# Moving the operands of a matmul stream by 64 bytes: where `u`, the weight ring and the block sums lie modulo 256 bytes

## Chip, cores, metric

One core of a Trainium2 chip runs one program. The metric is the device time of one execution in microseconds; the time of a kernel is the median of its runs.

## What is computed

One layer of a decoder block on 512 tokens of width 1024, in float32, with three sub-layers that each start from a normalised and modulated `u`:

```python
mod = cond @ w_ada[l] + b_ada[l]
u = modulate(rmsnorm(h, g_norm_ffn1[l]), sh1, sc1)
h = h + 0.5 * gt1 * swiglu(u, w_ffn1_in[l], w_ffn1_out[l])
u = modulate(rmsnorm(h, g_norm_mix[l]), sh2, sc2)
h = h + gt2 * token_mixing(u, cos, sin, w_in[l], ...)      # pooling and dilated attention, gated
u = modulate(rmsnorm(h, g_norm_ffn2[l]), sh3, sc3)
h = h + 0.5 * gt3 * swiglu(u, w_ffn2_in[l], w_ffn2_out[l])
return rmsnorm(h, g_final)
```

`swiglu` is `(silu(u @ w1) * (u @ w2)) @ w_out` with an inner width of 2816 (22 tiles of 128). All matrices are float32.

## The kernel before, in words

Everything is kept transposed: features on the 128 partitions, the 512 tokens along the free dimension, so `h` and `u` are eight tiles of 128x512. Precision comes from splitting: every operand x is stored as a high part `hi` and a rest `lo` (type float32r), and a product is three matmuls into one PSUM bank: `hi·uh`, `hi·ul`, `lo·uh` (`mm3`, lines 323 to 325). The **stationary** operand of a matmul is a 128x128 weight tile, 512 bytes a partition, which a weight load brings in while the matmul before it runs; the **moving** operand is 512 or 256 columns of `u` (2048 or 1024 bytes a partition).

**The ring.** Weights come from HBM in chunks of mostly 128x1024 into `raw` buffers (or, for block sums of weights, `X`). ScalarE writes each chunk's high part into the ring `whi` (L280), VectorE the rest into `wlo` (L292). `plan` lists all chunks in the order of use; `room` gives each the next place in the ring, in pieces of 128 floats (`unit`): where a chunk runs over the ring's end, it is cut in two and each piece has its own two instructions. `look` keeps the splitting three or four chunks ahead of `take`, which hands the tiles to TensorE.

**Order of the work.** All queues are written out by hand. In time: the startup (`startup`, L1482 to 1486: eight k-tiles, each 8 banks x 3 matmuls of 512 columns); the first feed-forward layer (ffn1): four pairs of inner tiles with 512-column matmuls (`ffn_pair`), seven `duo`s, and after each of five parts a stretch of output matmuls over the products `HI`/`HK` (512 columns); the mixing layer (mix); the second feed-forward layer (ffn2).

A `duo` makes two pairs of inner tiles with seven block products (`product`, L710 to 712) in place of eight, by sums of blocks of `u` and of the weights. A product is 24 matmuls of 256 columns. The moving operands of the seven, in order: `UH`/`UL`, `S0`, `S1`, `UH`/`UL`, `S2`, `UH`/`UL`, `UH`/`UL`, where S0 to S2 are the sums of blocks of `u` (`SH`/`SL` in the trace), made once for each feed-forward layer.

At the seams between the layers the tokens go in two halves of 256 columns: `out_tail` makes the last output tiles of a layer (for all its `ms`, first the left half, then the right half with the same weights) while the next norm starts on the left half, and `head` makes the first four input tiles of the next layer in the same way. In between stand the norm's sum over features (`stats_t`, L409) and its spreading (`spread`, L419), both small matmuls. `out_end` is the same for the end of the program. These are the "half tiles".

**Where the operands lie.** Tiles of a pool lie one behind the other, so addresses follow from the order and the sizes. In the built program `whi` starts at byte 13440 and `wlo` at 42112 of a partition, both 128 modulo 256; the ring's length (7168 floats) and a weight tile (512 bytes) are multiples of 256, so **every weight tile lies at 128 modulo 256**. `HI`, `HK`, `MH`, `ML`, `PH`, `YH` (moving operands of output stretches) lie at 128. `UH` starts at 87616 and `UL` at 104768, both 64; 16 floats more are reserved in each, and `place_u` moves the views by `U_AT` floats when a layer's norm begins:

```python
U_AT = (0, 16, 0)      # layer 0: ffn1, 1: mix, 2: ffn2
```

So `u` lies at 64 in ffn1 and ffn2, and at 128 in mix. S0 lies at 128; a pad of 48 floats behind it puts S1 and S2 at 64. Below, "equal" means that the moving operand and the weights of a matmul have the same address modulo 256, "64 apart" that the moving operand lies 64 bytes before the weights.

Of the kernel before, what the change touches and what calls it, by code (L numbers as in the profile page):

```python
# [8 lines left out]
F32 = mybir.dt.float32  # L9
F32R = mybir.dt.float32r  # L10
# [4 lines left out]
P = 128  # L15
T = 512
HT = 256
D = 1024
KT = 8
# [91 lines left out]


FIRST = 4
RING = 7 * 1024


U_AT = (0, 16, 0)

PLAIN = {0: 8, 2: 4}
PARTS = ((0, 4), (4, 8), (8, 12), (12, 16), (16, 22))  # L120
# [3 lines left out]
def pairs_before(n, part):  # L124

    k1 = PARTS[part][1]
    return k1 if part + 1 == len(PARTS) or (n == 2 and part == 0) else k1 + 2


def chunk_widths():  # L130
    outs = [D] * (KT // 2 * (len(PARTS) - 1)) + [(FT - PARTS[-1][0]) * P] * KT
    f1 = [2 * FIRST * P] * KT + [D] * (2 * (FT - FIRST)), outs
    mix = [D] * 20 + [D, D] + [D, D, 4 * P] * (KT - 1) + [4 * P] + [D] * KT
    return f1, mix, ([D] * (2 * FT), outs)


class Kernel:
# [6 lines left out]
    def plan(self):  # L144
        (i1, o1), mix, (i2, o2) = chunk_widths()
        self.chunks = []
        for name, ws in (("wf1i", i1), ("wf1o", o1), ("wmix", mix), ("wf2i", i2), ("wf2o", o2)):
            off, rec = 0, []
            for w in ws:
                rec.append((name, off, w))  # L150
                off += P * w
            self.chunks.append(rec)
        f1i, f1o, mx, f2i, f2o = self.chunks


        self.loads, self.order, self.last = [], [], {}

        def plain(recs):
            for r in recs:
                n = len(self.loads)  # L160
                self.loads.append(r)
                self.last[n] = len(self.order)
                self.order.append((r[2], n, ("raw", n), None))

        def blocks(recs):
            n = len(self.loads)
            self.loads.extend(recs)
            r11, r12, r22, r21 = (("raw", n + i) for i in range(4))
            x0, x1 = ("x", 0), ("x", 1)
            for need, src, make in ((0, r11, None), (1, x0, (x0, r12, r11)), (2, x1, (x1, r22, x0)), (3, r21, None),  # L170
                                    (3, r12, (r12, r22, r12)), (3, r22, None), (3, x0, (x0, r21, x1))):
                for j, x in enumerate((r11, r12, r22, r21)):
                    if x == src or (make and x in make):
                        self.last[n + j] = len(self.order)
                self.order.append((D, n + need, src, make))

        def ffn(n, ins, outs, first):
            j, at = first, 0
            if first:
                plain(ins[:KT])  # L180
                at = KT
            for part, (k0, k1) in enumerate(PARTS):
                while j < pairs_before(n, part):
                    if j < PLAIN[n]:
                        plain(ins[at:at + 2])
                        j, at = j + 1, at + 2
                    else:
                        blocks(ins[at:at + 4])
                        j, at = j + 2, at + 4
                plain(outs[part * KT // 2:(part + 1) * KT // 2] if part + 1 < len(PARTS) else outs[-KT:])  # L190

        ffn(0, f1i, f1o, FIRST)
        base = len(self.order)
        plain(mx)
        ffn(2, f2i, f2o, 0)
        self.fetched = self.done = self.made = 0
        self.pos, self.held, self.retired, self.half = 0, None, [], None
        self.at, self.start, self.top = {}, {}, 0
        self.buf = {}
        self.units = {base + i: 2 * P for i in (4, 5)}  # L200
        self.units.update({base + i: T for i in range(16, 20)})
# [33 lines left out]
    def room(self, i, held):  # L235


        w, u, at, pieces = self.order[i][0], self.unit(i), self.top, []
        for c in range(0, w, u):
            if at % RING + u > RING:  # L240
                at += RING - at % RING
            o = at % RING
            if pieces and pieces[-1][0] + pieces[-1][1].stop - pieces[-1][1].start == o:
                pieces[-1] = (pieces[-1][0], slice(pieces[-1][1].start, c + u))
            else:
                pieces.append((o, slice(c, c + u)))
            at += u
        low = min((self.start[j] for j in range(held, i)), default=self.top)
        return (pieces, at) if at - low <= RING else None

# [201 lines left out]
        self.nc.vector.scalar_tensor_tensor(self.UL[k][:, hs], t[:, hs], S, self.UH[k][:, hs],  # L452
                                            op0=OP.add, op1=OP.subtract)

    def place_u(self, n):
        self.UHv, self.ULv = (x[:, U_AT[n]:U_AT[n] + KT * T] for x in (self.UHall, self.ULall))
        self.UH, self.UL = ([x[:, k * T:(k + 1) * T] for k in range(KT)] for x in (self.UHv, self.ULv))

    def norm_steps(self, n, hs):

        t, done = {}, [0]

        def upto(k):
            while done[0] <= min(k, KT - 1):
                i = done[0]
                if i == 0:
                    t[0] = self.norm_a(n, 0, hs)
                if i + 1 < KT:
                    t[i + 1] = self.norm_a(n, i + 1, hs)
                self.norm_b(n, i, hs, t.pop(i))  # L470
                done[0] += 1
        return upto
# [9 lines left out]
    def out_tail(self, ms, ksrc, gate, nxt, squares):  # L482


        nc = self.nc
        tiles, starts = {}, {}
        A, Bh = slice(0, HT), slice(HT, T)
        step = None
        self.held = self.pos
        for h, hs in enumerate((A, Bh)):  # L490
            for m in ms:
                bank = self.nb()
                if h == 0:
                    starts[m] = self.pos
                    tiles[m] = ksrc(m)
                    starts[m + 1] = self.pos
                if h == 0 and m == ms[0]:
                    nc.scalar.preload_act_table(AF.Sqrt)
                if self.done < self.pos + 4:
                    self.split_hi()  # L500
                ks = tiles[m]
                for i, (hi, lo, uh, ul) in enumerate(ks):
                    if h == 1 and m == ms[1] and i == 3:
                        self.stats_t(self.B[6], A)
                    if h == 1 and m == ms[2] and i == 1:
                        self.spread(self.B[6], A)
                        self.place_u(nxt)
                        step = self.norm_steps(nxt, A)
                        step(0)
                    self.mm3(bank[:, hs], hi, lo, uh[:, hs], ul[:, hs], i == 0, i == len(ks) - 1)  # L510
                s = squares(m)[:, :HT]
                self.tail_step(m, hs, bank, gate, s)
                if h == 1:
                    self.held = starts[m + 1]
                    if step:
                        step(1 if m != ms[-1] else 3)
                self.split_lo()
                nc.vector.tensor_tensor(self.acc[:, hs], self.acc[:, hs], s, op=OP.add)
                self.fetch()
        self.stepA = step  # L520
# [171 lines left out]
    def step(self):  # L692

        self.now += 1
        due = [f for t, f in self.put if t <= self.now]
        self.put = [x for x in self.put if x[0] > self.now]
        for f in due:
            f()
# [105 lines left out]
    def open_sums(self):  # L804
        st = ExitStack()
        bp = st.enter_context(self.tc.tile_pool(name="fs", bufs=1))
        self.S = []
        for i in range(3):
            self.S.append([bp.tile([P, 4 * HT], F32R, name=f"S{x}{i}") for x in "HL"])
            if i == 0:  # L810
                bp.tile([P, 48], F32, name="padb")
        self.S.append([x.rearrange("p (k t) -> p k t", k=KT)[:, :4, HT:] for x in (self.UHv, self.ULv)])
        return st

# [520 lines left out]
    def build(self):  # L1335
# [6 lines left out]
        tl = lambda n, w, dt=F32: per.tile([P, w], dt, name=n)  # L1342
        self.free = [tl(f"raw{i}", CW) for i in range(3)]

        self.hi, self.lo = tl("whi", RING, F32R), tl("wlo", RING, F32R)
        self.vecs = tl("vecs", 106)
        self.H = [tl(f"H{k}", T) for k in range(KT)]
        self.UHall = tl("UH", KT * T + 16, F32R)
        cst, self.eps = tl("cst", 163), tl("eps", 1)
        self.ULall = tl("UL", KT * T + 16, F32R)  # L1350
        self.place_u(0)
        self.AR = tl("AR", 2 * T)
        self.acc, self.R = self.AR[:, :T], self.AR[:, T:]
        self.mod, self.part = tl("mod", 72), tl("part", 1)
# [197 lines left out]
```

## Time and profile before

| | |
|---|---|
| median of 3 runs | 1021.69 us |
| the runs | 1021.69, 1025.06, 1021.38 us |
| profiled execution, own time | 1025.08 us |
| its span | 1023.3 us |
| its granted TensorE clock | 0.998 |
| matmuls | 6364, as many weight loads |

A "busy" figure adds up the time of instructions. A matmul's own duration is longer than its distance to the next one, since matmuls are pipelined: how fast a stretch goes is read from the distance between the starts of two matmuls and the number of matmuls from one to the other, which the code gives.

### The profile page before, as it was taken

How to read it: one execution, taken by the hardware profiler on the slowest of the kernel's cores; microseconds unless marked ns; L12 is line 12 of the kernel's file. 1: busy time of each engine (PE TensorE's matmuls, PEld its weight loads, DVE VectorE, ACT ScalarE, POOL GpSimd, SP SyncE). 2: the span in 40 equal slices, each digit the busy share in tenths (PEclk: the TensorE clock that was granted, in tenths of full speed). 3: DMA queues.
4: the chain of work that ended last, by engine and by line, in shares of the span. 5: the costliest groups of instructions: out<-in, count | busy, mean ns of one | idle time of the engine just before them, and what ended most of it. 6: DMA issues, size and time to landing. Idle time of an engine off the chain costs nothing.

```text
span 1023.3 us, 15508 instructions
## 1 busy us (share of the span) xinstructions
PE 1012.1 (99%) x6364; PEld 914.9 (89%) x6364; DVE 753.2 (74%) x1082; ACT 434.8 (42%) x638; POOL 26.0 (3%) x30
## 2 busy tenths in 40 slices
PE   8999999999999999999999999999999999999997
PEld 7888898989999899889988888998899899998997
DVE  6969879889786777779446776577787776676754
ACT  5453352534445552334314333454365354352552
POOL 0000000000000000006100000000000000000001
PEclk9999999999999999999999999999999999999999
DMA  8856365555533513222154774322244234241312
GB/s 315 285 177 256 112 238 162 172 162 188 165 115 106 157 35 103 62 83 83 32 185 156 268 263 127 104 63 72 94 155 135 83 103 145 84 144 45 112 32 83
DMA packets 43113, 139.60 MB, mean 136 GB/s; under 512 B 4897, under 2 KB 8225, under 8 KB 43042
## 3 DMA queue, kind: packets, MB, share of 16 engines
q1 hardware_dynamic: 42354, 137.95, 41.3%
q8 instruction: 50, 0.82, 0.3%
q10 hardware_dynamic: 688, 0.66, 0.2%
q14 instruction: 21, 0.17, 0.1%
HBM read 135.82 MB, written 2.77 MB: 135 GB/s over the span
## 4 chain that ended last, share of the span: by engine, by line
PE 95%; DVE 3%; DMA 1%; ACT 0%; issue 0%; DVEq 0%; ACTq 0%
PE bank L323 17%; PE bank L324 17%; PE bank L325 17%; PE bank L710 10%; PE bank L712 10%; PE bank L711 10%; PE bank L1486 1%; PE bank L1484 1%; PE bank L1482 1%; PE bank L1080 1%; PE bank L1259 1%; PE bank L1411 1%; PE bank L1260 1%; PE bank L1261 1%; PE bank L1028 1%; PE bank L1057 1%
## 5 line engine op out<-in xcount | busy, mean ns | idle before, releaser
L292 DVE TENSOR_TENSOR wlo<-raw,whi 128x1024 fp32r<-128x1024 f32 (+2 forms) x151 | 175.5, 1165 | 69.0 <-ACT whi L280 68.8
L280 ACT ACTIVATE whi<-raw 128x1024 fp32r<-128x1024 f32 (+2 forms) x151 | 150.4, 1003 | 42.6 <-DVE raw L228 39.8
L323 PE MATMUL bank<-UH,whi 128*128 128x512 f32 (+1 forms) x432 | 159.0, 368 | 0.0
L324 PE MATMUL bank<-UL,whi 128*128 128x512 f32 (+1 forms) x432 | 154.9, 359 | 0.2 <-DVE UL L452 0.2
L325 PE MATMUL bank<-UH,wlo 128*128 128x512 f32 (+1 forms) x432 | 154.9, 359 | 0.0
L323 PE MATMUL bank<-HI,whi 128*128 128x512 f32 (+1 forms) x406 | 146.8, 362 | 0.0
L324 PE MATMUL bank<-HK,whi 128*128 128x512 f32 (+1 forms) x406 | 146.5, 361 | 0.0
L325 PE MATMUL bank<-HI,wlo 128*128 128x512 f32 (+1 forms) x406 | 146.5, 361 | 0.0
L710 PE MATMUL bank<-UH,whi 128*128 128x256 f32 x512 | 141.6, 277 | 0.0
L711 PE MATMUL bank<-UL,whi 128*128 128x256 f32 x512 | 141.6, 277 | 0.0
L712 PE MATMUL bank<-UH,wlo 128*128 128x256 f32 x512 | 141.6, 277 | 0.0
L292 DVE TENSOR_TENSOR wlo<-X,whi 128x1024 fp32r<-128x1024 f32 (+2 forms) x88 | 104.4, 1188 | 39.5 <-ACT whi L280 39.3
L710 PE MATMUL bank<-SH,whi 128*128 128x256 f32 x384 | 107.1, 279 | 0.3 <-ACT u L717 0.3
L711 PE MATMUL bank<-SL,whi 128*128 128x256 f32 x384 | 106.9, 278 | 0.0
L712 PE MATMUL bank<-SH,wlo 128*128 128x256 f32 x384 | 106.9, 278 | 0.0
L280 ACT ACTIVATE whi<-X 128x1024 fp32r<-128x1024 f32 (+2 forms) x88 | 89.3, 1028 | 33.1 <-DVE X L228 32.1
L711 PEld LDWEIGHTS bank<-UL,whi 128*128 128x128 f32 x512 | 96.1, 188 | 0.3
L710 PEld LDWEIGHTS bank<-UH,whi 128*128 128x128 f32 x512 | 96.1, 188 | 0.3
L712 PEld LDWEIGHTS bank<-UH,wlo 128*128 128x128 f32 x512 | 96.4, 188 | 0.0
L325 PEld LDWEIGHTS bank<-UH,wlo 128*128 128x128 f32 x432 | 81.3, 188 | 12.8
L324 PEld LDWEIGHTS bank<-UL,whi 128*128 128x128 f32 x432 | 81.5, 189 | 12.3 <-issue 0.5
L323 PEld LDWEIGHTS bank<-UH,whi 128*128 128x128 f32 x432 | 81.4, 189 | 11.9 <-issue 0.5
(225 smaller groups left out, 1748.5 us busy)
## 6 DMA issues: line engine op xcount, KB each, us to landing
ada<-wada SPq DMA_DIRECT2D x47, 512.0 KB, 5.0
raw<-wmix SPq DMA_DIRECT2D x44, 512.0 KB, 3.9
raw<-wf1i SPq DMA_DIRECT2D x34, 512.0 KB, 4.5
raw<-wf2i SPq DMA_DIRECT2D x30, 512.0 KB, 3.6
X<-wf2i SPq DMA_DIRECT2D x14, 512.0 KB, 3.5
cs<-wada SPq DMA_DIRECT2D x12, 512.0 KB, 3.5
AR<-wada SPq DMA_DIRECT2D x12, 512.0 KB, 3.9
raw<-wf2o SPq DMA_DIRECT2D x12, 512.0 KB, 3.6
```

The source lines that it names most:

```text
L280: self.nc.scalar.activation(self.hi[:, y], r[:, x], AF.Copy)
L292: self.nc.vector.tensor_tensor(self.lo[:, y], r[:, x], self.hi[:, y], op=OP.subtract)
L323: M(ps, hi, uh, start=start, stop=False)
L324: M(ps, hi, ul, start=False, stop=False)
L325: M(ps, lo, uh, start=False, stop=stop)
L710: M(o, hi, uh, start=start and p == 0 and k == 0, stop=False, skip_group_check=True)
L711: M(o, hi, ul, start=False, stop=False, skip_group_check=True)
L712: M(o, lo, uh, start=False, stop=k == 3, skip_group_check=True)
L1028: M(S[:, o + i * P:o + i * P + P], qz[:, (2 * i + h) * P:(2 * i + h + 1) * P], k[:, toks], start=True, stop=True)
L1057: nc.tensor.transpose(b[:, i * P:i * P + P], p[:, i * P:i * P + P], self.ident)
L1080: M(o, pt[:, blk * P:blk * P + P], v, start=i == 0, stop=i == len(srcs) - 1)
L1259: M(b, self.UH[k][:, c::4], hi, start=k == 0, stop=False)
```

## The change

It moves operands only; every engine issues the same work in the same order, except that chunks are cut at other places.

- `u` lies at 128 modulo 256 in all three layers; `place_u` and `U_AT` go, the pads stand ahead of `UH` and `UL`.
- The ring is 128 floats longer. `plan` collects in `shifted` the chunks that are to lie 16 floats (64 bytes) further on, at 192 modulo 256: all weights of block products; of ffn1's output the last three tiles, of mix's output the last two, of ffn2's output the last four (those of `out_tail` and `out_end` without the first tile of each); the four tiles of mix's `head` and of ffn2's `head`. `room` puts a chunk at its residue.
- S0 moves to 192, where the weights of block products now lie; S1 and S2 lie at 128.

```diff
-RING = 7 * 1024
-U_AT = (0, 16, 0)
+RING = 7 * 1024 + 128
+SHIFT = 16
...
+        self.shifted = set()
...
         def blocks(recs):
             n = len(self.loads)
+            self.shifted.update(range(len(self.order), len(self.order) + 7))
...
+        def shift(i):
+            self.shifted.update(range(len(self.order) - i, len(self.order)))
...
                     if j < PLAIN[n]:
                         plain(ins[at:at + 2])
+                        if n and j < 2:
+                            shift(2)
...
         ffn(0, f1i, f1o, FIRST)
+        shift(3)
         base = len(self.order)
         plain(mx)
+        self.shifted.update(range(base, base + 4))
+        shift(2)
         ffn(2, f2i, f2o, 0)
+        shift(4)
...
         w, u, at, pieces = self.order[i][0], self.unit(i), self.top, []
+        shift = SHIFT if i in self.shifted else 0
+        at += (shift - at) % 64
         for c in range(0, w, u):
             if at % RING + u > RING:
-                at += RING - at % RING
+                at += RING - at % RING + shift
...
-    def place_u(self, n):
...
-                        self.place_u(nxt)
...
         for i in range(3):
+            if i < 2:
+                bp.tile([P, (SHIFT, 64 - SHIFT)[i]], F32, name=f"padb{i}")
             self.S.append([bp.tile([P, 4 * HT], F32R, name=f"S{x}{i}") for x in "HL"])
-            if i == 0:
-                bp.tile([P, 48], F32, name="padb")
...
-        self.UHall = tl("UH", KT * T + 16, F32R)
+        tl("pad0", 16)
+        self.UHv = tl("UH", KT * T, F32R)
         cst, self.eps = tl("cst", 163), tl("eps", 1)
-        self.ULall = tl("UL", KT * T + 16, F32R)
+        tl("pad1", 16)
+        self.ULv = tl("UL", KT * T, F32R)
```

In the two built programs the residues of the float32r matmuls (moving, weights) are, with their counts:

| matmuls | columns | before | after | count |
|---|---|---|---|---|
| startup, and pairs of ffn1 and ffn2 outside `head` | 512 | 64, 128 | 128, 128 | 480 |
| `head` of mix, and the output half tiles but the first of each seam | 256 | 128, 128 | 128, 192 | 540 |
| block products with `u`, S1, S2 | 256 | 64, 128 | 128, 192 | 2304 |
| block products with S0 | 256 | 128, 128 | 192, 192 | 384 |
| `head` of ffn2 | 256 | 64, 128 | 128, 192 | 192 |
| all others | both | unchanged | unchanged | 2046 |

More of the change, by code (lines that the diff above doesn't have):

```diff
@@ L453, in norm_b @@
                                             op0=OP.add, op1=OP.subtract)
-    def place_u(self, n):
-        self.UHv, self.ULv = (x[:, U_AT[n]:U_AT[n] + KT * T] for x in (self.UHall, self.ULall))
-        self.UH, self.UL = ([x[:, k * T:(k + 1) * T] for k in range(KT)] for x in (self.UHv, self.ULv))
     def norm_steps(self, n, hs):
@@ L1347, in build @@
         self.H = [tl(f"H{k}", T) for k in range(KT)]
-        self.UHall = tl("UH", KT * T + 16, F32R)
+        tl("pad0", 16)
+        self.UHv = tl("UH", KT * T, F32R)
         cst, self.eps = tl("cst", 163), tl("eps", 1)
-        self.ULall = tl("UL", KT * T + 16, F32R)
-        self.place_u(0)
+        tl("pad1", 16)
+        self.ULv = tl("UL", KT * T, F32R)
+        self.UH, self.UL = ([x[:, k * T:(k + 1) * T] for k in range(KT)] for x in (self.UHv, self.ULv))
         self.AR = tl("AR", 2 * T)
```

## The prediction

> **What bounds the kernel now.** The page first: is there an engine that never rests?
>
> ```profile
> span 1023.3 us, 15508 instructions
> PE 1012.1 (99%) x6364; PEld 914.9 (89%) x6364; DVE 753.2 (74%) x1082; ACT 434.8 (42%) x638; POOL 26.0 (3%) x30
> PE 95%; DVE 3%; DMA 1%; ACT 0%; issue 0%; DVEq 0%; ACTq 0%
> ```
>
> TensorE is busy for 99% of the span and makes up 95% of the chain that ended last. The waits of TensorE are few:
>
> ```profile
> PE bank L1404 <- ACT cond L1402: 3.3, 1, 3.3
> PE bank L710 <- ACT u L717: 0.3, 1, 0.3
> PE bank L409 <- ACT ut L480: 0.3, 1, 0.3
> PE bank L1057 <- ACT prob L1045: 0.3, 1, 0.3
> PE bank L324 <- DVE UL L452: 0.2, 1, 0.2
> ```
>
> That is the whole list, 4.4 us, 3.3 of it before the first real matmul. No row names `whi`, `wlo` or a DMA of weights. So the time is a number of matmuls times the distance from one start to the next, and the question is what sets that distance. The timeline answers it. First the same code in two layers, the right half of `head`: 8 k-tiles x 4 banks x 3 = 96 matmuls of 256 columns, in mix (u and weights equal, both at 128) and in ffn2 (64 apart); two rows each, the first matmul and the one after the last, and from the groups of the same stretches one row each:
>
> ```profile
> 378.81 0.28 PE L323 MATMUL bank<-UH,whi 128*128 128x256 f32 x1
> 390.33 0.28 PE L1209 MATMUL bank<-whi,UH 128*128 128x256 f32 x1
> 684.35 0.28 PE L323 MATMUL bank<-UH,whi 128*128 128x256 f32 x1
> 695.23 0.39 PE L323 MATMUL bank<-UH,whi 128*128 128x512 f32 x1
> L323 PE MATMUL bank<-UH,whi 128*128 128x256 f32 x32 | 9.1, 283 | 0.0
> L323 PE MATMUL bank<-UH,whi 128*128 128x256 f32 x30 | 8.3, 276 | 0.0
> ```
>
> 11.52 / 96 = 120.0 ns when equal, 10.88 / 96 = 113.3 ns when 64 apart; each matmul's own duration differs by the same 7 ns (283 and 276). At 512 columns it is the other way round. The rows are the starts of an output stretch (equal, 72 matmuls up to the next row), of ffn1's pairs (64 apart, 96 matmuls up to the third row), and of two gate tiles of mix, whose moving operand is `u` too (equal, 48 matmuls):
>
> ```profile
> 92.55 0.39 PE L323 MATMUL bank<-HI,whi 128*128 128x512 f32 x1
> 108.87 0.39 PE L323 MATMUL bank<-UH,whi 128*128 128x512 f32 x1
> 131.27 0.28 PE L710 MATMUL bank<-UH,whi 128*128 128x256 f32 x1
> ...
> 542.14 0.39 PE L323 MATMUL bank<-UH,whi 128*128 128x512 f32 x1
> 553.02 0.39 PE L323 MATMUL bank<-PH,whi 128*128 128x512 f32 x1
> ```
>
> 16.32 / 72 = 226.7 ns and 10.88 / 48 = 226.7 ns when equal, 22.40 / 96 = 233.3 ns when 64 apart. So 512 columns want equal addresses, 256 columns want 64 bytes between, and either mismatch costs 6.6 to 6.7 ns a matmul. That is what the change acts on.
>
> There is a third pace. The first four products of a duo behind an output stretch, 24 matmuls from row to row (`UH`, S0, S1, `UH`):
>
> ```profile
> 172.26 0.28 PE L710 MATMUL bank<-UH,whi 128*128 128x256 f32 x1
> 175.09 0.28 PE L710 MATMUL bank<-SH,whi 128*128 128x256 f32 x1
> 177.96 0.29 PE L710 MATMUL bank<-SH,whi 128*128 128x256 f32 x1
> 180.70 0.28 PE L710 MATMUL bank<-UH,whi 128*128 128x256 f32 x1
> ```
>
> 2.83 / 24 = 117.9 ns for `UH`, although it is 64 apart; 2.87 / 24 = 119.6 for S0 (equal); 2.74 / 24 = 114.2 for S1, which has a few slow starts in it. The pace thus has a memory: coming from 512 columns, a stretch 64 apart runs in a middle gait until a product with equal addresses ends it.
>
> **The change, part by part.** The counts stand in the groups by form; what share of a row is meant follows from the code:
>
> ```profile
> L1482 PE MATMUL bank<-UH,whi 128*128 128x512 f32 x64 | 16.3, 397 | 0.0
> L323 PE MATMUL bank<-UH,whi 128*128 128x512 f32 x304 | 122.9, 404 | 0.0
> L323 PE MATMUL bank<-UH,whi 128*128 128x256 f32 x128 | 36.1, 282 | 0.0
> L323 PE MATMUL bank<-HI,whi 128*128 128x256 f32 x108 | 30.9, 286 | 0.0
> L323 PE MATMUL bank<-MH,whi 128*128 128x256 f32 x48 | 13.7, 286 | 0.0
> L710 PE MATMUL bank<-UH,whi 128*128 128x256 f32 x512 | 141.6, 277 | 0.0
> L710 PE MATMUL bank<-SH,whi 128*128 128x256 f32 x384 | 107.1, 279 | 0.3 <-ACT u L717 0.3
> ```
>
> (1) *512 columns become equal.* Startup 64 x 3, and of the 304 the pairs of ffn1 (4 pairs x 2 x 8 = 64) and ffn2 (2 x 2 x 8 = 32), x 3: 480 matmuls x 6.6 ns = **-3.2 us**. That the startup goes slow today shows in the chain, where eight matmuls are one piece, 1.87 / 8 = 233.8 ns, from the first to the last:
>
> ```profile
> 20.05 1.87 PE bank L1482 x8
> 62.99 1.87 PE bank L1486 x8
> ```
>
> (2) *Half tiles come 64 apart.* Mix's `head` 64 of the 128, `HI` 84 of 108, `MH` 32 of 48, x 3: 540 x 6.7 ns = **-3.6 us**.
>
> (3) *Block products keep their relation.* 2304 matmuls go from 64/128 to 128/192, S0's 384 from 128/128 to 192/192. If only the distance counts: 0. S0 stays at 120 ns, and stays the one that ends the middle gait.
>
> (4) *What comes back.* The middle gait: ffn1's first product after the pairs now follows equal 512 columns, 24 x 4.6 = 0.1 us; between `stats_t` and `spread` of four seams stand 12, 12, 18 and 18 half-tile matmuls, which in ffn2's `head` today also run slow (676.95 to 678.12, ten matmuls, 117):
>
> ```profile
> 676.95 0.28 PE L324 MATMUL bank<-UL,whi 128*128 128x256 f32 x1
> 678.12 0.28 PE L325 MATMUL bank<-UH,wlo 128*128 128x256 f32 x1
> ```
>
> 60 x 4 ns = 0.25 us. Some eight new entries from one relation to the other, 0.02 us each by S1 above (2.74 against 24 x 113.3 = 2.72): 0.15 us. And at the start of ffn2's `head` TensorE waits for the norm (the L452 row above); the 21 `MH` matmuls between `spread` and that point get 0.14 us faster, and the wait longer by as much. Together **+0.6 us**.
>
> (5) *Thirty chunks more are cut in two* by the longer ring, on ScalarE and VectorE each:
>
> ```profile
> L280 ACT ACTIVATE whi<-raw 128x1024 fp32r<-128x1024 f32 x130 | 135.9, 1050 | 42.6 <-DVE raw L228 39.8 <-DMA raw<-wmix 2.5 <-DMA raw<-wf1i 0.2
> L292 DVE TENSOR_TENSOR wlo<-raw,whi 128x1024 fp32r<-128x1024 f32 x130 | 158.9, 1224 | 55.6 <-ACT whi L280 55.4
> L292 DVE TENSOR_TENSOR wlo<-raw,whi 128x512 fp32r<-128x512 f32 x12 | 8.1, 688 | 8.0 <-ACT whi L280 8.0
> L280 ACT ACTIVATE whi<-raw 128x512 fp32r<-128x512 f32 x12 | 7.3, 624 | 0.0
> ```
>
> Two halves cost ScalarE 2 x 624 - 1050 = 198 ns more, VectorE 2 x 688 - 1224 = 152 ns. Cover: TensorE takes a chunk in 24 x 113.3 = 2.7 us, VectorE splits it in 1.2, three or four chunks ahead, and TensorE never waited for a weight. I take 0; uncovered it would be 30 x 152 = 4.6 us.
>
> Sum: -3.2 - 3.6 + 0.6 = **-6.2 us**. Against the profiled execution's own time, 1025.08 (span 1023.3), that is 1018.9. This execution was like the slowest of the three runs (1025.06); the median is 1021.69, so the forecast is 1021.69 - 6.2 = **1015.5 us**. What sets the 3.4 us between runs the trace doesn't show.
>
> A rule speaks against all of this: the Trainium skill, "SBUF — State Buffer", section "Who interferes with whom", says that TensorE has two independent read ports and never waits on anyone. By that, weight loads and moving operands could not disturb each other and addresses would not matter. The 120.0 against 113.3 ns above differ in nothing but address, so the trace disagrees; what would follow is the third rival.
>
> **Rivals.** (a) *The moving operand's own start decides, not the distance.* In this trace all weights lie at 128, so "64 apart" and "u at 64" can't be told apart; 128/192 is not in it. Then block products with `u`, S1 and S2 turn slow (2304 x 6.7 = +15.4 us), ffn2's `head` too (192 x 6.7 = +1.3), S0 at 192 turns fast (-2.6), half tiles gain nothing, (1) stays (-3.2): +10.9, **1032.6 us**, decided from the first block product on. Against it: the sign turns with the number of columns, and the same addresses go at 113.3 or 117.9 depending on what ran before, which speaks for two streams meeting. Chance 0.09.
> (b) *S0 at 192/192 no longer ends the middle gait:* the 2304 stay at 117.9, +10.6 against -6.2 + 1.4 for half tiles that gain less: **1027.5 us**. Chance 0.03.
> (c) *Pace belongs to the stretch, not the address:* nothing changes, **1021.7 us**. Against it: the same `head` at two paces. Chance 0.05.
> (d) *The cut chunks come through:* up to +4.6 us, **1020.1 us**. VectorE's idle time and the missing waits speak against it. Chance 0.13.
>
> **How the numbers follow.** The forecast has 0.70. 0.5% (5.1 us) is about what a measurement of this kernel tells from no change; 6.2 is little more, and if the middle gait or the waits take 1.1 us extra the result is "same", for which I put 0.10 of the 0.70. Faster 0.60, same 0.10 + 0.05 + 0.13 = 0.28, slower 0.12. Range: the forecast less 2.7 (an undisturbed median, no losses of (4), and some run to run), up to 1021.8 to take in (c) and (d): 1012.8 to 1021.8; (a) and (b) stay outside.
>
> **What would show it.** After: the startup's pieces of eight at 1.81 us; `head` of mix at 113.3 ns a start, L323 `HI` and `UH` 128x256 at 276 in place of 283; L710 `UH` still 277. If L710 `UH` x512 reads 283 it is (a), if 281 (b); if it reads 277 and TensorE's list of waits has rows for `whi` or `wlo`, (d). Wrong altogether if mix's `head` stays at 120.

## The result and the profile after

The changed kernel takes 1017.59 us, the median of 8 runs (1016.63 to 1020.22), beside 1022.31 us for the kernel before in 8 runs (1021.38 to 1025.06): ratio 0.9952, interval 0.994 to 0.9965, or -4.7 us. The two profiled executions differ by about as much, 1025.08 and 1020.22 us. The forecast was -6.2 us and 1015.5.

The head of the page, as shown of before:

```profile
span 1018.4 us, 15580 instructions
PE 1007.5 (99%) x6364; PEld 913.3 (90%) x6364; DVE 756.1 (74%) x1112; ACT 437.2 (43%) x668; POOL 26.2 (3%) x30
PE 94%; DVE 4%; ACT 0%; issue 0%; DMA 0%; DVEq 0%; ACTq 0%
```

TensorE is still what bounds the kernel, and the thirty chunks more that are cut stand there: VectorE 1082 to 1112 instructions, 753.2 to 756.1 us. The whole list of TensorE's waits says whether anyone met them:

```profile
PE bank L1416 <- ACT cond L1414: 3.3, 1, 3.3
PE bank L1067 <- ACT prob L1055: 0.3, 1, 0.3
PE bank L423 <- ACT ut L490: 0.3, 1, 0.3
```

No row for `whi` or `wlo`. So here too the time is matmuls times distance. From the groups by form, in the order of the rows of before (`mm3` is now L337 to 339, the product L719 to 721, the startup L1494 to 1498), and from the chain a middle piece of the startup:

```profile
L1494 PE MATMUL bank<-UH,whi 128*128 128x512 f32 x64 | 15.9, 391 | 0.0
L337 PE MATMUL bank<-UH,whi 128*128 128x512 f32 x304 | 122.3, 402 | 0.0
L337 PE MATMUL bank<-UH,whi 128*128 128x256 f32 x128 | 36.0, 281 | 0.0
L337 PE MATMUL bank<-HI,whi 128*128 128x256 f32 x108 | 30.6, 283 | 0.0
L719 PE MATMUL bank<-UH,whi 128*128 128x256 f32 x512 | 141.6, 277 | 0.0
L719 PE MATMUL bank<-SH,whi 128*128 128x256 f32 x384 | 107.1, 279 | 0.1
...
34.37 1.81 PE bank L1498 x8
```

512 columns of `u` went down (397 to 391, 404 to 402, pieces of eight 1.87 to 1.81 us), block products stayed (277, 279). The half tiles `HI` should read 276 and read 283 (286 before), and mix's and ffn2's `UH` together 281 where 282 stood. The timeline tells them apart. The right half of mix's `head`, 96 starts; then in ffn1's output the 54 starts of the tiles that are 64 apart, up to the return to the first tile; and 30 starts of the same kind behind `spread`:

```profile
375.09 0.28 PE L337 MATMUL bank<-UH,whi 128*128 128x256 f32 x1
385.97 0.28 PE L1219 MATMUL bank<-whi,UH 128*128 128x256 f32 x1
...
347.61 0.28 PE L337 MATMUL bank<-HI,whi 128*128 128x256 f32 x1
353.97 0.28 PE L337 MATMUL bank<-HI,whi 128*128 128x256 f32 x1
...
359.85 0.28 PE L337 MATMUL bank<-HI,whi 128*128 128x256 f32 x1
363.25 0.28 PE L337 MATMUL bank<-UH,whi 128*128 128x256 f32 x1
```

10.88 / 96 = 113.3 ns: mix's `head` does what was forecast. 6.36 / 54 = 117.8 ns: these output tiles run in what the prediction called the middle gait, from the first start. 3.40 / 30 = 113.3 ns: behind `spread` they are fast. Same operands, same addresses.

And one place got slower, ffn2's `head` behind its `spread`: 144 starts up to the first matmul of 512 columns, first in the kernel before, then in the changed one:

```profile
678.81 0.36 PE L323 MATMUL bank<-UH,whi 128*128 128x256 f32 x1
695.23 0.39 PE L323 MATMUL bank<-UH,whi 128*128 128x512 f32 x1
...
674.35 0.36 PE L337 MATMUL bank<-UH,whi 128*128 128x256 f32 x1
691.40 0.39 PE L337 MATMUL bank<-UH,whi 128*128 128x512 f32 x1
```

16.42 / 144 = 114.0 ns before, a few slow starts at the entry included, and 17.05 / 144 = 118.4 ns now, the middle gait again. Added up over all starts of both traces, from the first k-tile of the startup to near the end (distances of before less distances of the kernel, in us; positive is time won; the later columns belong to the experiments):

| part, starts | forecast | changed | run again | all 64 on | seam step back | 12 equal | 6 equal | 6 a duo |
|---|---|---|---|---|---|---|---|---|
| 512 columns of `u`, 480 | 3.2 | 3.13 | 2.85 | 3.12 | 3.15 | 3.09 | 3.08 | 3.13 |
| mix's `head`, 192 | 1.28 | 1.18 | 1.18 | 1.19 | 1.10 | 1.08 | 1.11 | 0.46 |
| output half tiles, 348 | 2.33 - 0.25 | 1.01 | 1.01 | 1.01 | 1.88 | 1.88 | 1.88 | 1.88 |
| ffn2's `head`, 192 | -0.14 | -0.76 | -0.11 | -0.14 | -0.12 | -0.12 | -0.12 | -0.12 |
| block products, 2688 | -0.1 | 0.07 | 0.09 | 0.08 | 0.09 | 1.80 | 2.08 | 2.51 |
| all other, and entries | -0.15 | -0.07 | -0.18 | -0.10 | -0.20 | -0.28 | -0.31 | -0.21 |
| together | 6.2 | 4.56 | 4.84 | 5.16 | 5.90 | 7.46 | 7.72 | 7.65 |

(In the first four kernels the row of block products holds 0.25 us of a single distance, 582 ns at 243.6 us in the trace of before and 326 to 331 since: the L710 row in the list of waits of before, which the list of after no longer has. The last 10 of the 348 half tiles lie behind the last start counted. In the run again the row of 512 columns is lower because its very first distance is 572 ns, 313 in the changed kernel. Numbers are rounded.)

### The profile page after: what moved, and what is told of

Its sections match the earlier page's. It is cut to its first block, busy times and chain, and to the rows that moved or that the text cites. A ratio compares the mean times of both kernels' runs of the same rounds, so it can differ in the third digit from the quotient of the medians.

```text
span 1018.4 us, 15580 instructions
## 1 busy us (share of the span) xinstructions
PE 1007.5 (99%) x6364; PEld 913.3 (90%) x6364; DVE 756.1 (74%) x1112; ACT 437.2 (43%) x668; POOL 26.2 (3%) x30
## 4 chain that ended last, share of the span: by engine, by line
PE 94%; DVE 4%; ACT 0%; issue 0%; DMA 0%; DVEq 0%; ACTq 0%
PE bank L337 17%; PE bank L338 17%; PE bank L339 17%; PE bank L719 10%; PE bank L721 10%; PE bank L720 10%; PE bank L1494 1%; PE bank L1496 1%; PE bank L1498 1%; PE bank L1090 1%; PE bank L1269 1%; PE bank L1423 1%; PE bank L1270 1%; PE bank L1271 1%; PE bank L1038 1%; DVE wlo L306 1%
## 5 line engine op out<-in xcount | busy, mean ns | idle before, releaser
L306 DVE TENSOR_TENSOR wlo<-raw,whi 128x1024 fp32r<-128x1024 f32 (+6 forms) x173 | 177.4, 1037 | 67.6 <-ACT whi L294 67.1
L294 ACT ACTIVATE whi<-raw 128x1024 fp32r<-128x1024 f32 (+6 forms) x173 | 152.3, 899 | 40.6 <-DVE raw L240 39.0
L337 PE MATMUL bank<-UH,whi 128*128 128x512 f32 (+1 forms) x432 | 158.3, 366 | 0.0
L337 PE MATMUL bank<-HI,whi 128*128 128x512 f32 (+1 forms) x406 | 146.6, 361 | 0.0
L719 PE MATMUL bank<-UH,whi 128*128 128x256 f32 x512 | 141.6, 277 | 0.0
L306 DVE TENSOR_TENSOR wlo<-X,whi 128x1024 fp32r<-128x1024 f32 (+4 forms) x96 | 105.3, 1103 | 39.0 <-ACT whi L294 38.7
L719 PE MATMUL bank<-SH,whi 128*128 128x256 f32 x384 | 107.1, 279 | 0.1
L294 ACT ACTIVATE whi<-X 128x1024 fp32r<-128x1024 f32 (+4 forms) x96 | 89.9, 958 | 32.1 <-DVE X L240 28.9
L719 PEld LDWEIGHTS bank<-UH,whi 128*128 128x128 f32 x512 | 96.1, 188 | 0.3
L339 PEld LDWEIGHTS bank<-UH,wlo 128*128 128x128 f32 x432 | 81.3, 188 | 12.1
L337 PEld LDWEIGHTS bank<-UH,whi 128*128 128x128 f32 x432 | 81.2, 188 | 11.3 <-issue 0.5
```

The lines of the kernel that those rows point to most:

```text
L294: self.nc.scalar.activation(self.hi[:, y], r[:, x], AF.Copy)
L306: self.nc.vector.tensor_tensor(self.lo[:, y], r[:, x], self.hi[:, y], op=OP.subtract)
L337: M(ps, hi, uh, start=start, stop=False)
L339: M(ps, lo, uh, start=False, stop=stop)
L719: M(o, hi, uh, start=start and p == 0 and k == 0, stop=False, skip_group_check=True)
```

## The experiments

Below, "core" is the time between the same two matmuls as in the table, which leaves out what lies ahead of the first k-tile: 991.59 us before, 987.03 after.

**The first block sum without its pads.** All of S0 to S2 at 128, 64 apart from their weights:

```diff
-            if i < 2:
-                bp.tile([P, (SHIFT, 64 - SHIFT)[i]], F32, name=f"padb{i}")
```

> S0 at 128 modulo 256, so 64 bytes before its weights like every other moving operand of the block products; nothing else differs from the changed kernel. Theory (the pace has a memory, and the 24 equal matmuls of S0 are what ends the middle gait that an output stretch leaves behind): each of the 16 duos now stays in the middle gait, 2304 matmuls go from 113.3 to 117.7 ns (+10.1 us) and S0's 384 from 119.6 to 117.7 (-0.7 us): 1027 us against the changed kernel's 1017.6. Rival (no memory, each matmul's pace follows its own addresses, S0 is merely slow where it lies): S0's 384 go from 119.6 to 113.3 (-2.4 us), the rest stays: 1015.2 us.

Measured: 1024.58 us, ratio 1.0021 (1.0007 to 1.0034), block products 7.10 us longer than before. The timeline, 24 starts from row to row (S0, S1), and a `UH` product later on:

```profile
129.24 0.28 PE L719 MATMUL bank<-SH,whi 128*128 128x256 f32 x1
132.06 0.28 PE L719 MATMUL bank<-SH,whi 128*128 128x256 f32 x1
134.89 0.28 PE L719 MATMUL bank<-UH,whi 128*128 128x256 f32 x1
...
243.57 0.28 PE L719 MATMUL bank<-UH,whi 128*128 128x256 f32 x1
246.29 0.28 PE L719 MATMUL bank<-UH,whi 128*128 128x256 f32 x1
```

2.82 and 2.83 / 24 = 117.7 ns: without an equal product nothing ends the middle gait, and whole duos stay in it. The time came out 2.4 us under the expectation, and the trace has a place for most of it. The middle gait isn't held for good: behind two long distances, the second of 222 ns at 240.7 us, the pace fell to 113.3 (2.72 / 24) and stayed there for the 236 starts to the end of the stretch, 1.0 us. And the expectation had charged the first product of all eight stretches too, 192 starts that run at 117.8 in the changed kernel already, 0.8 us. The pads of S0 carry some 7 us of the changed kernel.

**Half tiles as before.** The calls of `shift` for the outputs and the set for mix's `head` go; ffn2's `head` keeps its own:

```diff
-        shift(3)
...
-        self.shifted.update(range(base, base + 4))
-        shift(2)
...
-        shift(4)
```

> The half tiles of the output stretches and of mix's head lie at 128 again (equal), block products and u as in the changed kernel. Theory (half tiles gained 120.0 to 117.7 ns before the seam's spread and 113.3 behind it, and in ffn2's head the middle gait and an earlier wait cost 0.5 us of that again): +1.1 us for the outputs, +1.1 us for mix's head, -0.5 to -0.6 us in ffn2's head: 1019.2 us, 1.6 us over the changed kernel. Rival (my forecast's own size, 540 x 6.7 ns less small change): +3 us or more, 1020.7 us. Rival (half tiles gave nothing): 1017.6 us. Groups: HI 128x256 back to 283 to 286 ns, ffn2's head at 113.3 or 117.7 ns a start tells whether its gait hangs on what came before.

Measured: 1018.96 us, ratio 0.9961 (0.9946 to 0.9975); the core is 1.51 us longer than that of the changed kernel, near the 1.6 us of the theory: half tiles win little. The theory had counted the loss in ffn2's `head` as theirs. It is absent here, but the run of the changed kernel again, below, is without most of it too.

**128 bytes apart.** `SHIFT = 32`.

> The moved chunks lie 128 bytes on in place of 64 (weights at 0, S0 at 0, u, S1, S2 at 128): the only change is the distance, 128 apart. Theory (two streams of reads that start together collide where they fall on the same place, with a period that only the distance modulo 256 sets): a pace of its own, unknown; the block products' 2304 and the half tiles' 732 tell it: 113.3 ns would leave 1017.6 us, 120.0 would give 1017.6 + 2304 x 6.7 + about 2 = 1035 us, 106.7 (one place less to collide) 1017.6 - 17 to -20 = 999 us. Rival (only equal against unequal matters): 1017.6 us, L719 and L337 at 276 ns as in the changed kernel.

Measured: 1030.57 us, ratio 1.0072 (1.0055 to 1.0088). In place of a steady pace the trace has a round of five, 115, 118, 122, 120 and 119 ns; in the output half tiles, 45 starts from row to row:

```profile
351.41 0.28 PE L337 MATMUL bank<-HI,whi 128*128 128x256 f32 x1
356.75 0.28 PE L337 MATMUL bank<-HI,whi 128*128 128x256 f32 x1
```

5.34 / 45 = 118.7 ns. Block products lose 11.34 us. So it is not equal against unequal, by which 1017.6 us was expected: the distance counts.

**64 bytes the other way.** `SHIFT = 48`: weights and S0 at 64, the moving operand 64 bytes behind its weights instead of before them.

> The moved chunks lie 192 bytes on, which is 64 bytes before the moving operand modulo 256 (weights and S0 at 64, u, S1, S2 at 128): the distance of the changed kernel with its sign turned. Theory (the two streams start together and run at different speeds, so the sign counts): a pace other than 113.3 ns in the block products, 106.7 or 120.0: 999 or 1035 us. Rival (only equal against unequal matters): 113.3 ns, 1017.6 us, and the half tiles in the middle gait of 117.7 ns behind an equal stretch as in the changed kernel.

Measured: 1027.26 us, ratio 1.004 (1.0023 to 1.0057), none of the times expected. S1, behind an equal S0, from row to row 24 starts; then 48 starts of output half tiles, straight from the entry behind the equal first tile:

```profile
131.92 0.28 PE L719 MATMUL bank<-SH,whi 128*128 128x256 f32 x1
134.75 0.28 PE L719 MATMUL bank<-UH,whi 128*128 128x256 f32 x1
...
349.14 0.28 PE L337 MATMUL bank<-HI,whi 128*128 128x256 f32 x1
354.58 0.28 PE L337 MATMUL bank<-HI,whi 128*128 128x256 f32 x1
```

S1 at 2.83 / 24 = 117.9 ns, half tiles at 5.44 / 48 = 113.3: each the reverse of the changed kernel, at the same distance. What the two kernels have in common is the step by which a stretch leaves the equal state. Where an operand's address goes *back* by 64 bytes (S0 to S1 in the changed kernel, moving operand 192 to 128; here the weights of the half tiles, 128 to 64), the fast gait of 113.3 ns follows. Where it goes *forward* (weights 128 to 192 in the changed kernel's half tiles; here moving operand 64 to 128 behind S0), the middle gait of 117.7. The next runs test that rule.

It is a rule for the way out of the equal state only. Behind `spread`, with no equal matmul in between, the two kernels differ as well; the 30 starts that took 3.40 us in the changed kernel:

```profile
361.10 0.28 PE L337 MATMUL bank<-HI,whi 128*128 128x256 f32 x1
364.64 0.28 PE L337 MATMUL bank<-UH,whi 128*128 128x256 f32 x1
```

3.54 / 30 = 118.0 ns, and so behind all five `spread`s of this kernel: there the side of the weights on which the moving operand lies seems to count.

**A step back at the seams.** Only the second tile of each output seam goes to 64; the others stay at 192:

```diff
...
+        self.back.add(len(self.order) - 3)
...
-        shift = SHIFT if i in self.shifted else 0
+        shift = 64 - SHIFT if i in self.back else SHIFT if i in self.shifted else 0
...
```

> Half tiles of ffn1's and ffn2's outputs and of the mix: only the second tile of each seam, the first one that is off, is laid 48 floats on instead of 16, so that its weights start at 64 instead of 192 (a step back from 128, not forward); the tiles after it stay at 192. Theory (a 256-column start gets to the fast gait when an operand steps 64 bytes back from the equal state, and to the middle gait when it steps forward): the first half and the 9 starts of the second half ahead of the statistics of that tile go from 117.7 to 113.3 ns: 87 starts x 4.4 = 0.38 us; the tiles that follow it in the first half (114 starts) keep the fast gait, or fall back to the middle one on the step from 64 to 192; so -0.4 to -0.9 us against the changed kernel. Rival (middle gait comes from the change of residue itself, whichever way): 0 +- 0.1 us. The time itself cannot settle this, the pace of these tiles in the trace does.

Measured: 1018.19 us, ratio 0.9952 (0.9936 to 0.9969), which settles nothing; the trace does. A tile at 192 behind the one at 64 (24 starts, 349.7 to 352.6 in the changed kernel):

```profile
347.35 0.28 PE L340 MATMUL bank<-HI,whi 128*128 128x256 f32 x1
350.07 0.28 PE L340 MATMUL bank<-HI,whi 128*128 128x256 f32 x1
```

2.72 / 24 = 113.3 ns where 117.8 stood. The fast gait is entered by the step back and carried on across the step from 64 to 192. Output half tiles win 1.88 us against 1.01: +0.87, the upper end of what was expected.

**The first sum's product first.** In each duo the entries of `UH` and S0 change places, with their copies:

```diff
...
-        for i, (bank, u, start) in enumerate(((A, blk(lo4, T1), True), (B, S[0], True), (A, S[1], False),
+        for i, (bank, u, start) in enumerate(((B, S[0], True), (A, blk(lo4, T1), True), (A, S[1], False),
...
```

> In each duo of block products the product of the first block sum goes first, ahead of the one of the first unsummed half (the two change places, with their copies; nothing else). The first sum lies at 128, equal to its weights, the other half a step back. Theory (the middle gait is entered straight from equal 512-column starts on operands 64 bytes apart, and left through an equal product): the first product runs at 120.0 as it does in second place, and the product after it at 113.3 instead of 117.7: some 9 stretches x 24 starts x 4.4 ns = 0.95 us less than the changed kernel, about 1016.6 us. Rival (what follows 512 columns is the middle gait for any operand, or the middle gait comes back after the first sum): no change in pace, 1017.6 us; and if the first sum is late when it is asked for first, each duo waits for it: 0.2 to 0.5 us each, 1020 us or more.

Measured: 1034.27 us, ratio 1.0105 (1.0088 to 1.0121). (Here the weight sum of the next block is written over one whose low part is still to be cut, so this kernel computes other values; the work is the same.) The gait went as the theory says, 21 starts of `UH` behind S0; but the time went to a wait, which the list of TensorE's waits names:

```profile
128.44 0.29 PE L719 MATMUL bank<-UH,whi 128*128 128x256 f32 x1
130.84 0.28 PE L719 MATMUL bank<-UH,whi 128*128 128x256 f32 x1
...
PE bank L719 <- ACT bank L726: 11.8, 16, 1.7
```

2.40 / 21 = 114.3 ns with the entry in it, 113.3 once it is past. And 16 waits, one a duo, 11.8 us of the 16.7 that block products lost against the changed kernel: S1's product adds to the bank that ScalarE has just begun to copy, and the product that hid this copy had been moved ahead of it. It is not the wait that the expectation had priced; an order written by hand hides copies that no wait shows. Out of the wait 13 of the 16 duos came at 113.3 ns, three at 117.8.

**Everything 64 bytes on.** A pad of 16 floats ahead of all tiles, all distances kept.

> A pad of 16 floats ahead of everything: all tiles and weights 64 bytes on, so u at 192, the weights at 0 and so on, each pair's distance as in the changed kernel. Theory (only the distance counts): 1017.6 +- 0.8 us, block products at 113.3, 512 columns at 226.7, the first sum at 120.0. Rival (an operand's own place counts, as with the first rival of the prediction): products that start at another residue go to 120.0 or 117.7; with all of them 8 us or more.

Measured: 1017.47 us, ratio 0.9946 (0.9928 to 0.9965). In the table the column is that of the changed kernel, row by row, but for ffn2's `head`. Distance and steps count, not the place.

**The changed kernel again.**

> The changed kernel itself, on the chip of the other three: 0.9952 of the kernel before, 1017.6 us; it is what the others are compared with, stage by stage. Both theories: the same.

Measured: 1017.36 us, ratio 0.9941 (0.9927 to 0.9955), core 986.75. In this execution ffn2's `head` kept the fast gait, over the 144 starts that took 118.4 ns in the other:

```profile
673.01 0.36 PE L337 MATMUL bank<-UH,whi 128*128 128x256 f32 x1
689.42 0.40 PE L337 MATMUL bank<-UH,whi 128*128 128x512 f32 x1
```

16.41 / 144 = 114.0 ns. So behind `spread` the same program takes one gait or the other, and 0.65 us of the 0.76 were peculiar to one execution.

**Equal starts at the head of a stretch.** If the gait is only a matter of entry, S0 need not be equal. The pads go; each of the 8 stretches of block products begins with some weight tiles at 128, and all its other weights lie at 64, a step back (with the seams as in the run with a step back there):

```diff
...
+            if self.order[-1][2][0] != 'x':
+                self.opens.add(len(self.order))
-            self.shifted.update(range(len(self.order), len(self.order) + 7))
+            self.back.update(range(len(self.order), len(self.order) + 7))
...
+        if i in self.opens:
+            shift = 0
         at += (shift - at) % 64
         for c in range(0, w, u):
+            if i in self.opens and c == 2 * u:
+                shift = 64 - SHIFT
+                at += shift
...
```

With `4 * u`, 12 equal starts:

> Built on the kernel that lays the second tile of each seam a step back. Each of the 8 stretches of block products begins with 4 of its 8 weight tiles (12 starts) at 128, equal to the moving operand; the other 4 and all later weights of the stretch lie at 64, a step back. The first block sum loses its pads and lies at 128 like the others, so that it too is 64 bytes from its weights and nothing in the stretch is equal again. Theory (the gait is set by how the equal state was left, and is kept while nothing disturbs it): 12 starts at 120.0, then 113.3 for the rest of the first product and for all others, the 16 products of the first sum with them: 16 x 24 x 6.7 = 2.6 us and 8 x 12 x 4.4 - 8 x 12 x 2.3 = 0.2 us less than without; some 1014.2 us, ratio to before 0.991. Rival (an equal product is needed now and then to hold the fast gait, or the step back does nothing after so few equal starts): the products go on at 117.7 as without the pads, 6 to 7 us more: 1024 us.

With `2 * u`, as shown, 6:

> As the kernel with 12 equal starts at the head of each stretch of block products, with 6 of them (2 of 8 weight tiles). Theory: if 6 equal starts suffice to leave what 512 columns left behind, 8 x 6 x 6.7 = 0.3 us less than with 12, some 1013.9 us; if the first starts after 512 columns are not yet in the equal gait (they ran at 116 to 121 in mixed order where the first sum came first), some or all stretches go on at 117.7, up to 1024 us. Rival (as with 12): 1024 us in any case.

Measured: 1014.91 us, ratio 0.9926 (0.9908 to 0.9944), and 1015.04 us, 0.9926 (0.9908 to 0.9945). Cores 984.13 and 983.87: 6 do, and each start less that is equal is time won. With 6, S0 (24 starts), then a product behind the wait of which TensorE's row stands here:

```profile
128.62 0.28 PE L729 MATMUL bank<-SH,whi 128*128 128x256 f32 x1
131.34 0.28 PE L729 MATMUL bank<-SH,whi 128*128 128x256 f32 x1
...
238.00 0.39 PE L729 MATMUL bank<-SH,whi 128*128 128x256 f32 x1 [0.30 <-ACT u L736]
...
PE bank L729 <- ACT u L736: 0.3, 1, 0.3
```

S0 runs at 2.72 / 24 = 113.3 ns where it took 120. Block products won 1.71 and 1.99 us on the run with a step back at the seams, not the 2.8 and 3.1 that were expected, and the difference has a place: the wait at 238.00, for the same copy of `u` as in the kernel before (its L717 row), knocked the pace from 113.3 to 117.7 ns, and with nothing equal behind it the remaining 240 starts of that stretch stayed there, 240 x 4.4 = 1.1 us.

That nothing equal came is not the whole of it. The kernel before has the same wait, and the same S2 product behind it:

```profile
244.18 0.39 PE L710 MATMUL bank<-SH,whi 128*128 128x256 f32 x1 [0.31 <-ACT u L717]
245.32 0.28 PE L710 MATMUL bank<-SH,whi 128*128 128x256 f32 x1
247.02 0.28 PE L710 MATMUL bank<-UH,whi 128*128 128x256 f32 x1
```

1.70 / 15 = 113.3 ns: it was back in the fast gait within a few starts, with nothing equal in between. There the moving operand lies 64 bytes before its weights, here 64 bytes behind them. At this place all seven traces with the moving operand before the weights go on at 113.3 ns, and all five with it behind them at 117.7. A kernel with equal starts at the heads and the moving operand before its weights was not run.

**Equal starts at the head of every duo.** The condition goes, so that a stretch that lost the fast gait gets it back; with 6 equal starts, and with 3 (`c == u`):

> As the kernel with 6 equal starts at the head of each stretch of block products, with 6 equal starts at the head of each of the 16 duos. In that kernel the matrix engine waited 0.3 us for the copy of u in one duo of ffn1 (its start at 238.0 us), and from there to the end of the stretch all starts took 117.7 ns (264 of them). Theory (a wait can drop the gait, and a few equal starts followed by the step back bring it back): that wait stays, the 72 starts to the end of its duo stay at 117.7, the 162 behind the next duo's equal starts run at 113.3: -0.71 us, against 8 more heads x 6 x 6.7 ns = +0.32 us; the stretch from the first k-tile to the last steps 0.4 us shorter, the median about the same (1014.6). Rival (the gait after a wait is fixed until 512 columns come): the second duo stays at 117.7, 0.3 us longer.

> As the kernel with 6 equal starts ahead of every duo, with 3 (one weight tile). Theory: 3 equal starts suffice (the pace was at 120 from the second equal start on), 16 x 3 x 6.7 = 0.32 us less than with 6; 1014.3 us. Rival (3 are too few to clear what 512 columns leave): some or all stretches run at 117.7, up to 2000 starts x 4.4 = 9 us more: 1016 to 1023 us.

Measured: 1014.76 us, ratio 0.9918 (0.9902 to 0.9934), and 1014.62 us, 0.9925 (0.9906 to 0.9944). The S0 product of the duo behind the disturbed one, 24 starts, first with 6, then with 3:

```profile
249.97 0.28 PE L728 MATMUL bank<-SH,whi 128*128 128x256 f32 x1
252.69 0.28 PE L728 MATMUL bank<-SH,whi 128*128 128x256 f32 x1
```

```profile
249.54 0.28 PE L728 MATMUL bank<-SH,whi 128*128 128x256 f32 x1
252.37 0.28 PE L728 MATMUL bank<-SH,whi 128*128 128x256 f32 x1
```

2.72 / 24 = 113.3 against 2.83 / 24 = 117.9. Six equal starts repair the pace; three (119, 119 and 120 ns) don't, though three (113, 119 and 121 ns) do at the head of a stretch, behind 512 columns. It is one such place in each kernel. Block products won 2.51 us with 6, +0.43 on the stretch-wise kernel, as worked out (0.71 - 0.32 = 0.39). The cores are alike all the same, 983.94 and 983.79: with 6, mix's `head` fell into the middle gait behind its `spread` this time, 0.46 in place of 1.11 us, as in ffn2's `head` of the changed kernel above.

These four kernels beat both others: some 1014.8 us, 7 to 8 us under the kernel before by cores (983.8 to 984.1 against 991.6) as by medians, and 2.3 to 3.2 us under the changed one by cores (986.4 to 987.0). By medians the latter difference is 2.3 to 3.0 us, but across runs on different chips and occasions, and the intervals of the ratios overlap, so the claim against the changed kernel rests on the cores of single executions. Among the four no difference is shown.

## Why the prediction was right, and where its sum was not

*(1) 512 columns become equal*: 3.13 us against 3.2. Right in size and place.

*(2) Half tiles come 64 apart*: mix's `head` 1.18 of 1.28; the output half tiles 1.01 of 2.3. This is where the sum failed, and the term that was mis-sized is the middle gait of **step (4)**. The prediction had read that this gait exists, that it comes from 512 columns and that an equal product ends it, and concluded that half tiles, which follow an equal tile of 256 columns, would be free of it but for the 60 between `stats_t` and `spread`. In fact some 250 of the 348 ran in it: an equal tile ends the middle gait, but the step forward out of it, 128 to 192, begins it anew. Where block products of the kernel before leave the equal state for 64 apart, it is by a step back (S0 to S1, moving operand 128 to 64), so the other case was not in the trace. The run with a step back at the seams shows it: entry by the other step, +0.87 us.

ffn2's `head` made the rest, -0.76 instead of -0.14, in the profiled execution; in the same kernel run again -0.11. Of the 1.64 us between 6.2 and 4.56 these two make 1.07 + 0.62 = 1.69. In executions without that accident 4.8 to 5.2 us are won between the same matmuls.

*(3) Block products keep their relation*: 0 forecast, 0.07 measured (-0.18 without the single distance named under the table, most of it the first product that (4) had counted), with S0 at 120.0 and S1 free of the middle gait. The run without pads shows that this was no side matter: 7 us hang on S0 moving along.

*(5) The cut chunks*: 30 more on each engine (the page's counts), no wait for a weight. Right.

*The rivals.* (a), the moving operand's own start: excluded by L719 `UH` at 277 ns, and by the run with everything 64 bytes on. (b), S0 at 192/192 ends nothing: it does end the middle gait, S1 behind it reads 114.2 ns and the product after that 113.3. (c), the pace belongs to the stretch: mix's `head` went from 120.0 to 113.3, so its strict form falls, though there was more in it than the 0.05 it got, since within one relation two paces exist and a stretch keeps the one it has. By the rule of the Trainium skill behind it ("SBUF — State Buffer", "Who interferes with whom": TensorE's read ports for the moving operand and for weight loads are independent of each other) their addresses should not matter to the pace. The runs disagree: eleven kernels that differ from before in addresses and pads, and in little else, run from 1014.6 to 1030.6 us. (d), the cut chunks: no trace of it.

*The range* took in its low end an undisturbed median without the losses of (4) and its high end (c) and (d); the result lies 2.1 us above the forecast and inside. 1.5 us of the 2.1 are the smaller gain; 0.6 come from the starting point, as the median of before was 1021.69 in three runs and is 1022.31 in eight. At -0.48% it stands at the bound between "faster" and "within 0.5%", where the forecast had put a tenth for just this mechanism ("if the middle gait or the waits take 1.1 us extra").

*The 3.4 us between runs*, which the prediction left open: between the traces such differences lie before the first k-tile. The kernels with 12 and 6 equal starts differ by 0.3 us in the core and by 3.1 in the span (1015.7 and 1012.6). One row of the windows, from 13 to 16 us (behind the length PE's busy time and its matmuls; the granted clock is third from the end), and the chain's first piece of the startup, with 12 equal starts and then with 6; below them the windows row of the changed kernel run again, from 16 to 19 us:

```profile
13.00:16.00 3.00, 3.00 (x15) 3.00 (x16) 1.12 (x6) 1.14 (x3) 0.00 (x0) 1.00 1.04 410
20.11 1.83 PE bank L1502 x8
```

```profile
13.00:16.00 3.00, 2.99 (x26) 2.80 (x26) 1.92 (x9) 1.30 (x3) 0.00 (x0) 1.00 1.03 410
16.89 2.14 PE bank L1502 x8
```

```profile
16.00:19.00 3.00, 3.00 (x15) 2.81 (x14) 3.00 (x6) 1.84 (x4) 0.00 (x0) 0.58 1.02 412
```

15 small matmuls against 26 in the same 3 us, 213 ns from start to start against 112, and the first k-tile 2.9 us later (its first start at 19.80 and 16.89). Over all profiled executions the first k-tile begins between 16.4 and 19.8 us. The granted clock reads 1.00 in both. In the run again, whose small matmuls go at 112 ns and then fall back to 213, it reads 0.58 over the row shown. The Trainium skill, "TensorE: Matmul & The Clock Gate", "What's actually happening", says that the array runs at half its clock until some 3.4 us of activity have released it, counted in windows that don't start with the kernel. The factor (213 against 112) and the 0.58 would fit; the clock column of the two kernels compared does not show it, and the slow pace lasts 7.6 us longer in one than in the other (to 19.7 us against 12.1), more than one such window. So it stays a reading.

## What to carry to other kernels

Where a stream of matmuls is the bound, read its pace as start to start over counted matmuls, stretch by stretch, and compare stretches that differ in nothing but the addresses of their operands. A pace seen in one stretch can depend on what ran before it, so before moving a term to another stretch check that the way in is the same too, not only the steady state. And where a stall can end the good state, ask what restores it: six equal starts a duo won 0.43 us of block products here, their own price taken off, which the time of the whole kernel doesn't show.

## What the runs showed of the hardware

- With 256 columns of float32r, weights and moving operand 64 bytes apart modulo 256, there are two steady paces at the same addresses, 113.3 and 117.7 ns; equal 120.0; 128 apart 118.7 in a round of five in the output half tiles, 118.5 to 120.3 in the block products. With 512 columns: equal 226.7, 64 apart 233.3 ns.
- Which of the two is taken, out of the equal state with 256 columns: a step of 64 bytes back gave 113.3 and a step forward 117.7 wherever it was tried, each with the weights and with the moving operand. Straight from equal 512 columns and behind `stats_t` always 117.7; from 512 columns that were 64 apart (the first block product of the kernel before) 113.8.
- Behind a disturbance it goes mostly with the side. Moving operand before the weights: 113.3 behind `spread` in 50 of 52 places over twelve traces, behind the wait or long distance near 240 us in all seven traces, and behind 13 of the 16 waits where S0's product came first. Moving operand behind the weights: 117.7 or 117.8 in all five places behind `spread` and in all five traces near 240 us. Why the exceptions are exceptions is not shown.
- 3 equal starts cleared what 512 columns leave, but not what a wait had left, in the one place where that was tried; 6 cleared both.
- 113.3, 120.0, 226.7 and 233.3 are 17, 18, 34 and 35 times 6.67 ns; 117.7 is no such multiple. What in the chip keeps this state is not shown by these runs.
